# A linear attention's output products in halves of the depth, in pairs on the two halves of the array's rows, with a PSUM bank for each half

## The chip, the cores and the metric

The kernel runs on one core of a Trainium2 chip, written in Bass and Tile. The metric is the device time of one execution in microseconds, median of the runs shown. Its result must agree with the reference in fp32.

## What is computed

One layer of a decoder: 1024 tokens of width 1024, a wide input projection, then two branches side by side, softmax attention with latent queries and keys (8 heads) and a gated linear attention (4 heads), a gated merge, an output product and gated embeddings. The part that matters here is the linear attention:

```python
def step(state, inp):                      # per head, chunk by chunk
    qi, ki, vi, bi = inp                   # bi: running sum of the log decay
    o_inter = einsum('bhcd,bhde->bhce', qi * exp(bi), state)
    ...
    attn = einsum('bhid,bhjd,bhijd->bhij', qi, ki, decay)
    o = o_inter + einsum('bhij,bhje->bhie', attn, vi)
    ...
```

The kernel takes chunks of 128 tokens. For each head and chunk the output is a sum of two products: the chunk's decayed scores times its values (depth 128, the chunk's tokens), and the decayed queries times the state that the earlier chunks left (depth 64, the head's width). The first chunk has no state.

## The kernel before

The dense products (`bank`, line 149) are made of three products each (`mm3`, lines 144 to 147: high by high, high by low, low by high part of the operands), 128 rows deep and 512 columns wide; a bank is 24 of them, or 8 steps of depth. They run as a stream of tiles (`stream`, line 158), the next tile's weights loaded one tile ahead (`load_w`: a DMA, a copy of the high part on ScalarE, line 127, and the low part on VectorE, line 128). The input projection's last 25 tiles fill the time of the linear attention, from 116 to 440 us: `steps` (line 733) runs `gla(t, h)` for the four pairs of a half `h` of the tokens and a pair `t` of heads, and after each `yield` in it one dense bank is issued (lines 740 and 741). The framework then puts the instructions of each engine in an order by a model of the time, so a bank may be moved a little; on each engine the order is fixed when the kernel runs.

A call of `gla` handles two heads and four chunks in ten steps. It makes the states (`pu`, line 586); the scores in six parts, merged into the tile `at` by VectorE (lines 637 and 641), each part by products on 64 rows, one head in rows 0 to 63 and the other in rows 64 to 127 (`cross`, line 555, alternates the heads, each head with a PSUM bank of its own); then, in one step, the outputs: for each head a PSUM bank `po`, and per chunk a product of `at` with the values (line 684, 128 rows) and one of `qe` with the state (line 700, 64 rows). ScalarE copies the bank out (line 702) and squares it with sums by token (line 706). The next step turns the sums into the norm's factor (`newton`, VectorE), the one after scales on GpSimd (line 717) and transposes back on TensorE (line 720).

PSUM has eight banks of 512 fp32 columns. In this stage (line 454) two are for dense products (`d`), four for two score tiles of two banks each (`L`), one for an output (`o`) and one for the rest (`u`: transposes, states). `o` is used once more, for the sums of a latent's norm (line 788).

Of the kernel before, what the change touches and what calls it, by code (L numbers as in the profile page):

```python
# [11 lines left out]
AF = mybir.ActivationFunctionType  # L12
# [4 lines left out]
P = 128  # L17
# [11 lines left out]
# columns of the packed gain vectors  # L29
V_IN, V_Q, V_KV, V_BGK, V_GLA, V_PLE, V_PG, V_FIN = 0, 8, 11, 13, 15, 16, 24, 32  # L30
NVEC = 40
# columns of the float constants
# [7 lines left out]
def _pieces(v):  # L40
    """v as a sum of two numbers of 12 bits and a float."""
    a = np.float64(v)
    out = []
    for _ in range(2):
        m, e = math.frexp(a)
        p = math.ldexp(round(math.ldexp(m, 12)), e - 12)
        out.append(p)
        a = a - p
    out.append(float(np.float32(a)))
    return out  # L50


def hybrid_kernel(tc, a, out):
# [3 lines left out]
    with ExitStack() as ctx:  # L57
# [72 lines left out]
        def split_gain(dst_hi, dst_lo, src, g):  # L130
            """the two parts of src * g, g per partition"""
            nc.scalar.activation(dst_hi, src, AF.Copy, scale=g)  # L132
            nc.vector.scalar_tensor_tensor(dst_lo, src, g, f(dst_hi), op0=ALU.mult, op1=ALU.subtract)  # L133
# [15 lines left out]
        def bank(get, hi, lo, w, c0, kts, xh, xl, h, evict, tag="d"):  # L149
            """out[w features, half h of the tokens] with the weights' k-tiles at c0 + kt * w."""  # L150
            ps = get(tag, "d")
            n = len(kts)
            for i, kt in enumerate(kts):
                c = slice(c0 + kt * w, c0 + kt * w + w)
                mm3(ps[:w], hi[:, c], lo[:, c], xh[kt][:, hs(h)], xl[kt][:, hs(h)], i == 0, i == n - 1)
            evict(h, ps)

        def stream(get, jobs, xh, xl, primed=None, ahead=1, order=None):
            """Dense tiles, the next one's weights always on their way; yields after the first
            load and after each bank.  # L160
            A job: (source, columns of a k-tile, k-tiles, evict)."""
# [25 lines left out]
        def newton(dst, ss, n, w):  # L187
            """dst = rsqrt(ss / n + EPS), [128, w]"""
# [14 lines left out]
        def newton1(dst, s1, s2, n):  # L203
            """dst = rsqrt((s1 + s2) / n), [128, 1]; v is half the argument, the iterates change sign"""
# [13 lines left out]
        def rstd_rows(get, tag, acc, n, r):  # L218
            """From acc[128, tokens] (sums of squares by partition) the rstd of token block tb in r[128, 8]."""
            pr = get(tag, "ss")  # L220
            for tb in range(8):
                nc.tensor.matmul(pr[:, tb : tb + 1], acc[:, tb * P : (tb + 1) * P], ones[:, 0:1], start=True, stop=True)
            newton(r, pr[:, :8], n, 8)

        def rstd_parts(r):
            """both parts of r [128, 8]"""
            rh, rl = small("rh", 8, F32R, bufs=2), small("rl", 8, bufs=2)
            nc.scalar.activation(rh, r, AF.Copy)
            nc.vector.tensor_tensor(rl, r, f(rh), op=ALU.subtract)
            return f(rh), rl  # L230

        def rstd_bcast(get, tag, parts, h):
            """[128, 512] in PSUM: rstd of each token of half h along the free axis, on every partition."""
# [20 lines left out]
        # =====================================================================  # L254
        # The input projection. Its operand is x * g; the token's rstd comes in
        # where a product leaves PSUM.
        # =====================================================================
# [14 lines left out]
        with tc.tile_pool(name="ps0", bufs=1, space=PSUM) as ps0:  # L272
# [20 lines left out]
            # the array reaches its full clock only under load: it gets some while the first loads are on their way  # L293
# [4 lines left out]
            # x * g in two parts, and the sums of squares  # L298
# [53 lines left out]
            # constants of the linear attention  # L352
# [4 lines left out]
            # the gate's second product in one pass: rows 64.. hold the operands' parts  # L357
            # (hi, hi, lo, lo) and (hi, lo, hi, lo)
# [10 lines left out]
            # gate chain: the running sums of log sigmoid within a chunk  # L369
# [22 lines left out]
            # rope tables: cos, and sin with its sign. A tile of rope's rows holds four heads'  # L392
            # first halves, then their second halves.
            cs = [alloc(F32, "cs") for _ in range(2)]

            def rope_tables():
# [23 lines left out]
                # the key's: parts in rows 0.. and 32.., halves of them in rows 64.. and 96..  # L420
# [12 lines left out]
            # values of the linear attention, by token  # L433
# [14 lines left out]
        # =====================================================================  # L448
        # Linear attention, between the tiles of the rest of the projection
        # =====================================================================  # L450
        with tc.tile_pool(name="psG", bufs=1, space=PSUM) as psG:
            gctx = ExitStack()
            gp = gctx.enter_context(tc.tile_pool(name="gtmp", bufs=NG))
            get = psum_pool({"d": (HALF, 2), "L": (S, 2), "o": (HALF, 1), "u": (HALF, 1)}, psG)
# [44 lines left out]
            # latents: raw, and their sums of squares  # L499
# [31 lines left out]
            def gla(t, h):  # L531
                """Pair of heads t, half h: four chunks of 128 tokens."""
# [34 lines left out]
                # decayed keys, by token, and the chunks' states  # L567
# [41 lines left out]
                # the chunks' own scores, transposed, level by level  # L609
# [43 lines left out]
                # neighbours and the diagonal  # L653
# [19 lines left out]
                # outputs by token, their norm, and back  # L673
                ss = small("gss", 8)
                oss = []
                prev = None
                for hd in range(2):
                    po = get("o", "o")
                    e0 = (2 * t + hd) * P
                    for c in range(4):  # L680
                        tb = 4 * h + c
                        cs = slice(c * P, (c + 1) * P)
                        st = states[c]
                        i1 = nc.tensor.matmul(
                            po[:, cs],
                            at[:, hd * HALF + c * P : hd * HALF + (c + 1) * P],
                            vtok(tb)[:, e0 : e0 + P],
                            start=True,
                            stop=st is None,
                        )  # L690
                        if c:
                            tc.add_manual_dep(
                                i1.ins,
                                prev.ins.name,
                                mybir.DependencyInfo(mybir.DependencyClass.NoSync, mybir.DependencyReason.DATA),
                                reason="one group at a time in a bank",
                            )
                        prev = i1
                        if st is not None:
                            prev = nc.tensor.matmul(po[:, cs], qe[rows(hd), cs], st[rows(hd), :], start=False, stop=True)  # L700
                    os_ = g2("os")
                    nc.scalar.activation(os_, po, AF.Copy)
# [45 lines left out]
            # the gated outputs in two parts  # L748
# [39 lines left out]
            kvh, kvl = finish_latent(get, "o", "L", "ckv", 256, V_KV)  # L788
# [8 lines left out]
        # =====================================================================  # L797
        # Softmax attention
        # =====================================================================
        with tc.tile_pool(name="psB", bufs=1, space=PSUM) as psB:  # L800
# [15 lines left out]
            def rope_queries(g):  # L816
                """Rope's rows of four heads' queries, in two parts to DRAM."""
# [18 lines left out]
            def make_pair(pr):  # L836
                """Queries and keys of two heads, without rope in rows 0.. of the first's and rows
                64.. of the second's; rope's rows 64..95, and 0..63 twice (the keys' halved)."""
# [35 lines left out]
            # values, by token, packed [hi | lo] per head  # L874
# [58 lines left out]
            def weighted(hn, hf, pq, sl, rc4):  # L933
# [3 lines left out]
                # the gate over the softmax's sums, these as rows by way of DRAM  # L937
# [65 lines left out]
            def parts(pr, h):  # L1003
                """both parts of heads' pair pr, half h"""
# [7 lines left out]
            # per-layer embeddings, by token, times their gain; half the norm's factor in re  # L1012
# [91 lines left out]
        # =====================================================================  # L1104
        # Merge, output product, gated embeddings, final norm
        # =====================================================================
        with tc.tile_pool(name="psC", bufs=1, space=PSUM) as psC:
# [7 lines left out]
            # x2 = x + merged @ w_out: its parts times the gain by feature, itself by token  # L1115
# [56 lines left out]
            def block(tb, b, c0, w, et):  # L1172
                """Columns c0 .. c0 + w of block b's; they start at column o of the row."""
# [28 lines left out]
            for tb in range(8):  # L1202
                # all but the row's last piece, and their sum with the guard's share
# [21 lines left out]
def _tiles(w, cols, width=P):  # L1225
    """[K, M] -> rows of m-tiles, each [128, K / 128 * width]: partition = k within its tile."""
# [30 lines left out]
def _layout(inputs):  # L1257
# [21 lines left out]
    # rope's columns, by four heads: the first halves, then the second halves  # L1279
# [35 lines left out]
```

## Time and profile before

| | us |
|---|---|
| three runs: median | 996.18 |
| lowest, highest | 995.36, 997.62 |
| span of the profiled execution | 995.6 |
| TensorE busy (matmuls) | 968.8 (97%) |
| VectorE busy | 585.0 (59%) |
| ScalarE busy | 413.4 (42%) |
| GpSimd busy | 127.8 (13%) |
| linear attention's stretch | 116 to 440 |

The time of a run is that of the whole execution; the span is from the first to the last instruction in the one execution that was profiled. A product in fp32 shows as two records of a matmul and two of a weight load. A matmul's record is longer than the distance to the next one, since they are pipelined: read distances from start to start.

### The profile page before, as it was taken

How to read it: one execution, taken by the hardware profiler on the slowest of the kernel's cores; microseconds unless marked ns; L12 is line 12 of the kernel's file. 1: busy time of each engine (PE TensorE's matmuls, PEld its weight loads, DVE VectorE, ACT ScalarE, POOL GpSimd, SP SyncE). 2: the span in 40 equal slices, each digit the busy share in tenths (PEclk: the TensorE clock that was granted, in tenths of full speed). 3: DMA queues.
4: the chain of work that ended last, by engine and by line, in shares of the span. 5: the costliest groups of instructions: out<-in, count | busy, mean ns of one | idle time of the engine just before them, and what ended most of it. 6: DMA issues, size and time to landing. Idle time of an engine off the chain costs nothing. (4 is left out here: it accounts for less than half of the span.)

```text
span 995.6 us, 13955 instructions
## 1 busy us (share of the span) xinstructions
PE 968.8 (97%) x5152; PEld 801.1 (80%) x5152; DVE 585.0 (59%) x1219; ACT 413.4 (42%) x800; POOL 127.8 (13%) x103
## 2 busy tenths in 40 slices
PE   7999999999999999999999999997999999999996
PEld 5787778887887788788888788886888778889985
DVE  6727764375364355342567568885756862238766
ACT  7316721332331332221233246785886432237333
POOL 2100000000000000001111022234454000000322
PEclk9999999999999999999999999998999999999999
DMA  7300111122232122130162844537146762135212
GB/s 277 93 22 22 64 43 43 58 80 86 75 106 79 60 85 75 54 114 24 54 204 89 230 131 121 150 94 180 59 149 212 245 221 74 43 106 181 74 64 106
DMA packets 47827, 105.68 MB, mean 106 GB/s; under 512 B 6736, under 2 KB 9616, under 8 KB 47760
## 3 DMA queue, kind: packets, MB, share of 16 engines
q1 hardware_dynamic: 47760, 104.81, 32.9%
q8 instruction: 40, 0.66, 0.3%
q14 instruction: 27, 0.22, 0.1%
HBM read 72.18 MB, written 25.20 MB: 98 GB/s over the span
## 5 line engine op out<-in xcount | busy, mean ns | idle before, releaser
L145 PE MATMUL d<-xh,wh 128*128 128x512 f32 x544 | 215.4, 399 | 3.1 <-ACT xh L132 3.0
L146 PE MATMUL d<-xl,wh 128*128 128x512 f32 x544 | 214.1, 394 | 0.1
L147 PE MATMUL d<-xh,wl 128*128 128x512 f32 x544 | 213.8, 394 | 0.1
L145 PEld LDWEIGHTS d<-xh,wh 128*128 128x128 f32 x544 | 102.7, 189 | 28.2 <-ACT xh L132 4.9
L128 DVE TENSOR_TENSOR wl<-wr,wh 128x1024 fp32r<-128x1024 f32 (+2 forms) x59 | 73.6, 1249 | 86.9 <-ACT wh L127 66.7
L146 PEld LDWEIGHTS d<-xl,wh 128*128 128x128 f32 x544 | 102.9, 189 | 22.0 <-DVE xl L133 0.8
L147 PEld LDWEIGHTS d<-xh,wl 128*128 128x128 f32 x544 | 102.7, 189 | 22.2 <-DVE wl L128 0.5
L127 ACT ACTIVATE wh<-wr 128x1024 fp32r<-128x1024 f32 (+4 forms) x81 | 76.3, 943 | 105.5 <-DMA wr<-in_w_in 35.8
L145 PE MATMUL pg<-wh,gh 128*128 128x256 f32 (+1 forms) x200 | 62.7, 314 | 0.0
L146 PE MATMUL pg<-wl,gh 128*128 128x256 f32 (+1 forms) x200 | 62.5, 313 | 0.0
L147 PE MATMUL pg<-wh,gl 128*128 128x256 f32 (+1 forms) x200 | 62.5, 313 | 0.0
L128 DVE TENSOR_TENSOR pt<-pt,pt 128x512 fp32r<-128x512 f32 (+1 forms) x96 | 51.5, 551 | 16.1 <-ACT pt L127 15.7
L924 ACT ACTIVATE p<-p,nm 128x128 f32<-128x128 f32 (+3 forms) x64 | 49.3, 772 | 21.8 <-DVE nm L914 21.7
L494 ACT ACTIVATE z<-z 128x512 f32<-128x512 f32 x32 | 20.1, 629 | 91.1 <-DVE z L466 85.3
L466 DVE TENSOR_TENSOR z<-d,rb 128x512 f32<-128x512 f32 x32 | 22.0, 688 | 50.9 <-PE d L147 50.9
L145 PE MATMUL d<-mh,wh 128*128 128x512 f32 x128 | 50.9, 400 | 0.6 <-ACT mh L127 0.6
L127 ACT ACTIVATE pt<-pt 128x512 fp32r<-128x512 f32 (+1 forms) x96 | 44.6, 485 | 15.5 <-PE pt L963 14.0
L146 PE MATMUL d<-ol,wh 128*128 128x512 f32 x128 | 50.1, 393 | 0.4 <-DVE ol L128 0.4
L147 PE MATMUL d<-mh,wl 128*128 128x512 f32 x128 | 50.2, 392 | 0.0
L147 PE MATMUL d<-oh,wh 128*128 128x512 f32 x128 | 50.0, 392 | 0.0
L146 PE MATMUL d<-ml,wh 128*128 128x512 f32 x128 | 49.9, 390 | 0.0
L145 PE MATMUL d<-oh,wh 128*128 128x512 f32 x128 | 49.9, 395 | 0.0
(262 smaller groups left out, 1938.5 us busy)
## 6 DMA issues: line engine op xcount, KB each, us to landing
wr<-in_w_in SPq DMA_DIRECT2D x33, 512.0 KB
d_ta<-z SPq DMA_DIRECT2D x16, 256.0 KB
d_tb<-z SPq DMA_DIRECT2D x16, 256.0 KB
tb<-d_tb SPq DMA_DIRECT2D x16, 256.0 KB
d_zb<-tb SPq DMA_DIRECT2D x16, 256.0 KB
d_e<-er SPq DMA_DIRECT2D x16, 256.0 KB
ta<-d_ta SPq DMA_DIRECT2D x16, 256.0 KB
zb<-d_zb SPq DMA_DIRECT2D x16, 256.0 KB
```

Source lines behind the costliest of these rows:

```text
L127: nc.scalar.activation(dst_hi, src, AF.Copy)
L128: (eng or nc.vector).tensor_tensor(dst_lo, src, f(dst_hi), op=ALU.subtract)
L145: nc.tensor.matmul(ps, lh, rh, start=first, stop=False)
L146: nc.tensor.matmul(ps, lh, rl, start=False, stop=False)
L147: nc.tensor.matmul(ps, ll, rh, start=False, stop=last)
L466: nc.vector.tensor_tensor(z, ps, rb[:, hs(h)], op=ALU.mult)
L494: nc.scalar.activation(z, z, AF.Tanh, scale=0.5)
L924: nc.scalar.activation(pt[:, :w], pt[:, :w], AF.Exp, bias=nm, scale=-1.0, accum_out=den)
```

## The change

The output step's PSUM bank per head becomes a tile of two banks for each half of the depth, `po[0]` and `po[1]`, taken from the `L` buffers: `po[k]` holds what rows `64k` to `64k + 63` contribute, one head in its first bank and the other in its second. The score product of depth 128 is divided in two of depth 64. Per chunk the order is head 0 on rows 0 to 63 and head 1 on rows 64 to 127; head 0 on rows 64 to 127 and head 1 on rows 0 to 63; then, where there is a state, each head's state product on its own rows. VectorE adds the two halves after ScalarE's copy of the first. The bank `o` goes to the dense products, which have three, and the latent's sums use `u`. In all other places the diff only takes out comments and docstrings.

```diff
-            get = psum_pool({"d": (HALF, 2), "L": (S, 2), "o": (HALF, 1), "u": (HALF, 1)}, psG)
+            get = psum_pool({"d": (HALF, 3), "L": (S, 2), "u": (HALF, 1)}, psG)
...
-                prev = None
+                po = [get("L", "o") for _ in range(2)]
+                prev = {}
+                for c in range(4):
+                    tb = 4 * h + c
+                    cs = slice(c * P, (c + 1) * P)
+                    st = states[c]
+                    for part in range(2 if st is None else 3):
+                        for hd in range(2):
+                            k2 = hd ^ (part == 1)
+                            r, hc = rows(k2), slice(hd * HALF + c * P, hd * HALF + (c + 1) * P)
+                            e0 = (2 * t + hd) * P
+                            lt, rt = (at[r, hc], vtok(tb)[r, e0 : e0 + P]) if part < 2 else (qe[r, cs], st[r, :])
+                            i1 = nc.tensor.matmul(po[k2][:, hc], lt, rt, start=part < 2, stop=part == 2 or st is None or k2 != hd)
+                            if (k2, hd) in prev:
+                                tc.add_manual_dep(
...
+                            prev[k2, hd] = i1
                 for hd in range(2):
-                    po = get("o", "o")
-                    e0 = (2 * t + hd) * P
-                    for c in range(4):
...
-                        i1 = nc.tensor.matmul(
-                            po[:, cs],
-                            at[:, hd * HALF + c * P : hd * HALF + (c + 1) * P],
-                            vtok(tb)[:, e0 : e0 + P],
-                            start=True,
-                            stop=st is None,
-                        )
...
-                        if st is not None:
-                            prev = nc.tensor.matmul(po[:, cs], qe[rows(hd), cs], st[rows(hd), :], start=False, stop=True)
                     os_ = g2("os")
-                    nc.scalar.activation(os_, po, AF.Copy)
+                    nc.scalar.activation(os_, po[0][:, hs(hd)], AF.Copy)
+                    nc.vector.tensor_tensor(os_, po[1][:, hs(hd)], os_, op=ALU.add)
...
-            kvh, kvl = finish_latent(get, "o", "L", "ckv", 256, V_KV)
+            kvh, kvl = finish_latent(get, "u", "L", "ckv", 256, V_KV)
```

## Rows read from the trace of the kernel before

**Rows 1.** The page: busy time by engine, and TensorE's busy tenths in 40 slices.
```profile
PE 968.8 (97%) x5152; PEld 801.1 (80%) x5152; DVE 585.0 (59%) x1219; ACT 413.4 (42%) x800; POOL 127.8 (13%) x103
...
PE   7999999999999999999999999997999999999996
```

**Rows 2.** Stretch, length; busy PE, PEld, DVE, ACT, POOL; granted clock; DMA share, GB/s.
```profile
116.00:440.00 324.00, 323.78 (x1877) 259.44 (x1876) 167.02 (x308) 99.12 (x194) 12.17 (x16) 1.00 0.21 72
```

**Rows 3.** Timeline of TensorE, outputs of half 0: start, length, instruction, merged count.
```profile
176.07 0.39 PE L147 MATMUL d<-xh,wl 128*128 128x512 f32 x1
...
177.25 0.49 PE L684 MATMUL o<-gqkv,at 128*128 128x128 f32 x2
...
178.08 0.49 PE L684 MATMUL o<-gqkv,at 128*128 128x128 f32 x2
...
178.92 0.50 PE L145 MATMUL d<-xh,wh 128*128 128x512 f32 x1
179.25 0.40 PE L146 MATMUL d<-xl,wh 128*128 128x512 f32 x1
```

**Rows 4.** The same timeline around a group of outputs of half 1.
```profile
327.31 0.39 PE L145 MATMUL d<-xh,wh 128*128 128x512 f32 x1
...
330.76 0.50 PE L146 MATMUL d<-xl,wh 128*128 128x512 f32 x1
331.10 0.40 PE L147 MATMUL d<-xh,wl 128*128 128x512 f32 x1
```

**Rows 5.** The same timeline around eight products of scores (16 records).
```profile
168.18 0.39 PE L145 MATMUL d<-xh,wh 128*128 128x512 f32 x1
...
168.63 0.39 PE L147 MATMUL d<-xh,wl 128*128 128x512 f32 x1
...
170.04 0.50 PE L145 MATMUL d<-xh,wh 128*128 128x512 f32 x1
170.38 0.39 PE L146 MATMUL d<-xl,wh 128*128 128x512 f32 x1
```

**Rows 6.** The timeline with windows that end early: the first records of two groups.
```profile
176.30 0.49 PE L684 MATMUL o<-gqkv,at 128*128 128x128 f32 x3
176.30 0.60 PE L684 MATMUL o<-gqkv,at 128*128 128x128 f32 x4
168.95 0.49 PE L559 MATMUL L<-rq,rk 64*128 64x128 f32 x4
168.95 1.05 PE L559 MATMUL L<-rq,rk 64*128 64x128 f32 x14
```

**Rows 7.** Groups by line, count, busy us, mean ns, idle time before and its releaser.
```profile
L702 ACT ACTIVATE os<-o 128x512 f32<-128x512 f32 x8 | 4.8, 599 | 30.1 <-PE o L700 30.1
L706 ACT ACTIVATE junk<-os 128x128 f32<-128x128 f32 x32 | 9.5, 299 | 0.2
L466 DVE TENSOR_TENSOR z<-d,rb 128x512 f32<-128x512 f32 x32 | 22.0, 688 | 50.9 <-PE d L147 50.9
```

**Rows 8.** Timelines of TensorE and GpSimd behind two groups of outputs.
```profile
186.68 0.50 PE L146 MATMUL d<-xl,wh 128*128 128x512 f32 x1
194.84 2.04 POOL L717 TENSOR_TENSOR os<-os,grs 128x512 f32<-128x512 f32 x2 [44.46 <-DVE grs L200]
...
416.11 0.50 PE L147 MATMUL d<-xh,wl 128*128 128x512 f32 x1
420.73 2.04 POOL L717 TENSOR_TENSOR os<-os,grs 128x512 f32<-128x512 f32 x2 [41.55 <-DVE grs L200]
426.68 0.60 PE L720 MATMUL oT<-ident,os 128*128 128x128 f32 x4
```

**Rows 9.** Waits by total: who waited for whom, us, times, longest.
```profile
DVE wl L128 <- PE o L684: 20.1, 2, 10.7
```

**Rows 10.** TensorE's longest wait in the softmax attention, and the stretch behind (as in 2).
```profile
690.33 0.42 PE L145 MATMUL s<-kh,qh 96*128 96x128 f32 x1 [5.17 <-DMA kl<-kl]
690.40:700.50 10.10, 9.48 (x37) 8.71 (x37) 5.75 (x21) 6.95 (x16) 6.67 (x4) 0.50 0.56 171
```

More of the change, by code (lines that the diff above doesn't have):

```diff
@@ L675, in gla @@
                 oss = []
-                prev = None
-                for hd in range(2):
-                    po = get("o", "o")
-                    e0 = (2 * t + hd) * P
-                    for c in range(4):
-                        tb = 4 * h + c
-                        cs = slice(c * P, (c + 1) * P)
-                        st = states[c]
-                        i1 = nc.tensor.matmul(
-                            po[:, cs],
-                            at[:, hd * HALF + c * P : hd * HALF + (c + 1) * P],
-                            vtok(tb)[:, e0 : e0 + P],
-                            start=True,
-                            stop=st is None,
-                        )
[L691 to L698, printed above, removed]
-                        if st is not None:
-                            prev = nc.tensor.matmul(po[:, cs], qe[rows(hd), cs], st[rows(hd), :], start=False, stop=True)
@@ new lines, in gla @@
+                po = [get("L", "o") for _ in range(2)]
[13 more added lines that the diff above has]
+                                tc.add_manual_dep(
+                                    i1.ins,
+                                    prev[k2, hd].ins.name,
+                                    mybir.DependencyInfo(mybir.DependencyClass.NoSync, mybir.DependencyReason.DATA),
+                                    reason="one group at a time in a bank",
+                                )
+                            prev[k2, hd] = i1
```

## The prediction

> **What bounds the kernel now.** I read the page first: TensorE's matmuls are busy for 97% of the span and of the forty slices only the first, the last and one at 685 to 710 us fall under 9 tenths, while VectorE is at 59% and ScalarE at 42% [rows 1]. Matmuls overlap in their pipeline, so "busy" alone doesn't prove a bound. The table by stages does better: in the linear attention's stretch, 116 to 440 us, TensorE is busy for 323.78 of 324.00 us at full granted clock, VectorE for 167 us and ScalarE for 99 us [rows 2]. In that stretch TensorE never waits for anything that counts; what stands in its queue sets the time. So a microsecond taken out of TensorE's queue there is a microsecond off the end, provided that nobody else then comes late, and that the later stages, where TensorE is as busy in nearly every slice [rows 1], are simply pushed forward.
>
> Next I read the output products one by one, in order of time. What counts is the distance from start to start, not the duration of a record. Each fp32 product shows as two records. Dense products follow each other by 0.225 us (168.18 to 168.63, with one more start between, is 0.45 us) [rows 5]. A group of output products (one head, four chunks) is bounded by the last dense start ahead of it and the second dense start behind it; two normal distances (0.45 us) are taken off.
>
> - Half 0 of the tokens, where the first chunk has no state and so no second product: 176.07 to 179.25 is 3.18 us, less 0.45 is 2.73 us [rows 3]. There are four such groups.
> - Half 1, with all eight products: 327.31 to 331.10 is 3.79 us, less 0.45 is 3.34 us [rows 4]. Four of these too.
>
> The sum is 4 x 2.73 + 4 x 3.34 = 24.3 us of the span's 995.6.
>
> Where do they go? Records of 128 rows that follow each other start every 0.11 us: the first three end 0.49 us after the group's start and the first four 0.60 us [rows 6]. A chunk with both products has four records and would take 0.44 us at that rate, but 177.25 to 178.08 is 0.83 us [rows 3]. The missing 0.39 us goes at the two places where the queue changes between a product on 128 rows (line 684) and one on 64 rows (line 700): about 0.2 us for each change of form, and there are 6 in a group of half 0 and 8 in one of half 1, counting the return to the dense products.
>
> **What the change takes and adds on TensorE.** The new group holds both heads. It has only products on 64 rows, those on rows 0 to 63 alternating in pairs with those on rows 64 to 127: per chunk 4 halves of the score product and 2 state products. That makes 22 products in half 0 and 24 in half 1, four groups in all. Every second neighbour is of the same half (the order is 0 1, 1 0, 0 1), but taken two by two each pair lies on different halves and in different PSUM banks.
>
> The trace has this form already: `cross` issues 8 products on 64 rows, heads alternating. From the last dense start (168.63) to the second one behind (170.38) is 1.75 us, less 0.45 is 1.30 us for the eight, both changes of form included [rows 5]. Within it, ten more records take 1.05 - 0.49 = 0.56 us [rows 6], so 0.056 us a record and 0.112 us a product, which is half of a 128-row product's. So a new group costs 1.30 + (22 - 8) x 0.112 = 2.87 us in half 0 and 1.30 + (24 - 8) x 0.112 = 3.09 us in half 1. Two of each: 11.9 us.
>
> TensorE gives back 24.3 - 11.9 = **12.4 us**. Cutting the score product in two halves earns nothing by itself: two halves at 0.112 cost what one whole product at two records of 0.11 costs. Of the 12.4 us about 3 are the 28 state products, which now run in pairs (28 x 0.11), and the rest is changes of form: 4 x 6 + 4 x 8 = 56 before, two for each new group, 8, after.
>
> Bounds: if nothing overlapped within a new group, a record would cost 0.11 us, and 44 or 48 records plus the 0.40 us of entry and exit (1.30 - 16 x 0.056) would be 5.24 and 5.68 us; together 21.8 us, a gain of 2.4 us. Above, nothing in the rows is faster than `cross`. I take `cross`, since the form (64x128), the alternation and the two banks are the same.
>
> **What it adds elsewhere.** ScalarE's eight copies of 0.60 us stay. VectorE gets eight additions of a 128x512 PSUM tile and an SBUF tile; the nearest row, the dense evictions of that shape, is 0.69 us [rows 7], so 5.5 us in a stretch where VectorE is free for 157 us. They cost nothing as long as two things hold. First, the squares (line 706) now wait for the addition and the ScalarE queue behind them waits too: what is queued there are the ScalarE half of weight splits and the tanh of dense evictions. The work that hides such delays is the dense products themselves. How much they hide a wait shows: VectorE stood 20.1 us in two pieces, 10.7 us the longer, in front of a weight split, for line 684's last reading of the score tile [rows 9], and TensorE still lost only 0.22 us in the whole stretch. So a delay of 0.7 us is covered; if that cover were gone, eight of them would cost 5.5 us, and I count 0. (The 20.1 us shrink too, since both heads now finish together.) Second, the transposes of line 720 must still find their operand ready; that is the rival below.
>
> PSUM: both `L` buffers are taken by the new output tile. They were last read by the fourth and fifth merges of scores, and the output products need the fifth merge anyway, so no new wait on entry. The next user of `L` is the next pair's first scores, four steps (four banks of dense work) later. The third `d` bank has no wait to remove, since TensorE waits for none [rows 2]; I count it at nothing. So is the move of the latent's sums to the bank `u`, long after its last user.
>
> **The rivals.**
>
> *The halves don't overlap in this order.* Twice per chunk two neighbours use the same rows. The trace's only example alternates strictly. The Trainium skill (TensorE: Matmul & The Clock Gate, What overlaps and what doesn't) says that weight loads overlap matmuls in flight only where the rows differ and that matmuls keep strict order; taken strictly, that speaks for this rival, and no row here shows the order 0 1 1 0. Time: 996.2 - 2.4 = 993.8 us. Against it: pairs counted from the chunk's start never share rows. 7 in 100.
>
> *The eviction becomes the bound.* The Trainium skill (TensorEngine Tiling, PSUM Bottleneck) warns that tiling speeds up TensorE and not the emptying of PSUM. In rows: the scaling on GpSimd began 194.84 - 186.68 = 8.2 us after the last output product in the slowest group and 420.73 - 416.11 = 4.6 us in the quickest [rows 8]. To that come the first head's copy and squares, which ran beside dense work between the two heads before (0.60 + 4 x 0.30 = 1.8 us by [rows 7]), two additions (1.4 us) and the first scaling itself (1.0 us): the first transpose can go 8.8 to 12.4 us after the products. Its cover was 426.68 - 416.11 = 10.6 us at least [rows 8] and is by the order of the steps two banks, 2 x 24 x 0.225 = 10.8 us, to which the 5 us of dense work that stood between the two heads may come. So at worst 1.5 to 2 us in some of four groups, a time of 984 to 990 us: 9 in 100.
>
> *Slower than before* by the same place: if the transposes were queued behind one bank only (5.4 us), TensorE would stand 3.4 to 7.0 us in each of four groups, 14 to 28 us, and the time would be 998 to 1012 us. It decides from 3.1 us of wait per group (12.4 / 4). Against it: the steps put two banks in between, and the shortest distance in the trace is 10.6 us. 3 in 100.
>
> *A later wait shifts.* In the softmax attention TensorE once stands 5.17 us for a copied key tile, and the granted clock is 0.50, the 1.2 GHz level, for 10 us from there [rows 10]. All of it moves forward with the rest, but the order there may come out a little different: without it up to 5 us of wait and the 5 us that half the clock costs less (974), with a second one 10 us more (994). 4 in 100 each way.
>
> **How the numbers follow.** Likeliest, 73 in 100: 12.4 us off. The profiled span is 995.6 us and the median of three runs 996.18, so 0.6 us lies around it; 996.2 - 12.4 = 983.8 us, its own range 981 to 987. The range of 8 in 10 reaches down to 979 (half of the later wait gone) and up to 992 (eviction waits, part of the overlap missing). A change within 0.2% (2 us), about what a measurement of this kernel can tell from none, needs the first rival at its worst or waits that eat the gain: 3 in 100. Slower: 3 in 100. Faster: 94 in 100.
>
> **What would show it.** The steps are right if the groups of output products come as four runs of 44 or 48 records on 64 rows that take 2.7 to 2.9 us from the first to the next dense start, with TensorE's work up to the end of the last group shorter by some 12 us and no wait ahead of line 720's transposes. Records 0.11 us apart would mean the first rival; gaps on TensorE ahead of the transposes the second. An equal or longer span with short groups would make the whole argument wrong: TensorE's queue would not have been the bound.

## The result and the profile after

The changed kernel takes 984.96 us (median of 4 runs, 983.49 to 988.31), the kernel before 995.77 us beside it. The ratio is 0.9893, 95% interval 0.9869 to 0.9916: about 1.1% faster. Forecast were 983.8 us and a range of 979 to 992. Two later repetitions of the changed kernel gave 987.9 and 984.84 us, ratios 0.991 and 0.9877.

The page of the changed kernel: busy time by engine, and TensorE's busy tenths in 40 slices.

```profile
PE 955.8 (97%) x5216; PEld 794.3 (81%) x5216; DVE 590.2 (60%) x1227; ACT 413.1 (42%) x800; POOL 128.1 (13%) x103
...
PE   7999999999999999999999999997999999999995
```

TensorE has 64 records more and 13 us less of busy time than in [rows 1]; its picture by slices is the same but for the last digit. That it still bounds the linear attention's stretch is read from its idle time there, below. VectorE has 5 us more, the eight additions.

The timeline of TensorE in the changed kernel (start, length, instruction, merged count; in brackets the wait before and what ended it): the last record of the stage before the linear attention, a group of outputs of each half, the first transposes behind one, the first record of the stage after, the product behind the long wait in the softmax attention, and a product at which the clock is back.

```profile
115.36 0.39 PE L147 MATMUL gv<-wh,xl 128*128 128x512 f32 x1
...
175.70 0.39 PE L147 MATMUL d<-xh,wl 128*128 128x512 f32 x1
176.01 1.16 PE L690 MATMUL o<-gqkv,at 64*128 64x128 f32 x16
177.01 0.39 PE L690 MATMUL o<-st,qe 64*128 64x128 f32 x4
...
178.67 0.50 PE L145 MATMUL d<-xh,wh 128*128 128x512 f32 x1
179.00 0.39 PE L146 MATMUL d<-xl,wh 128*128 128x512 f32 x1
...
193.32 0.60 PE L720 MATMUL oT<-ident,os 128*128 128x128 f32 x4
...
321.82 0.39 PE L145 MATMUL d<-xh,wh 128*128 128x512 f32 x1
325.02 0.50 PE L146 MATMUL d<-xl,wh 128*128 128x512 f32 x1
325.36 0.39 PE L147 MATMUL d<-xh,wl 128*128 128x512 f32 x1
...
508.57 0.39 PE L145 MATMUL v<-wh,ch 128*128 128x512 f32 x1
...
678.01 0.44 PE L145 MATMUL s<-kh,qh 96*128 96x128 f32 x1 [5.53 <-DVE pt L128]
...
688.14 0.48 PE L145 MATMUL s<-kh,qh 96*128 96x512 f32 x1
```

Read as [rows 3] and [rows 4] were, from the last dense start to the second dense start behind, less 0.45: 179.00 - 175.70 - 0.45 = 2.85 us in half 0, 325.36 - 321.82 - 0.45 = 3.09 us in half 1. All four groups together are 11.88 us, where the eight of before were 24.28. The same two outer records in the kernel before, and the last product:

```profile
115.70 0.39 PE L147 MATMUL gv<-wh,xl 128*128 128x512 f32 x1
...
521.05 0.40 PE L145 MATMUL v<-wh,ch 128*128 128x512 f32 x1
...
700.46 0.55 PE L145 MATMUL s<-kh,qh 96*128 96x512 f32 x1
```

Between the first two lies the whole linear attention with its dense work: 521.05 - 115.70 = 405.35 us before, 508.57 - 115.36 = 393.21 us after. The gain is there, 12.14 us. Below this distance is called the GLA stretch.

Two stretches of the changed kernel (length; busy PE, PEld, DVE, ACT, POOL; granted clock; DMA share, GB/s):

```profile
116.00:440.00 324.00, 323.77 (x1993) 262.13 (x1992) 174.62 (x319) 101.12 (x198) 12.13 (x16) 1.00 0.21 76
...
674.43:688.09 13.66, 9.42 (x35) 8.68 (x36) 6.03 (x21) 8.54 (x19) 7.28 (x4) 0.50 0.70 176
```

The first answers to [rows 2]: no wait has come in, at 0.23 us of idle time against 0.22. The second answers to [rows 10]: at the long wait the granted clock is at the 1.2 GHz level for 13.66 us here, for 10.2 us in the profile of before. The longer stretch holds no more work: 3.58 us of it (674.43 to 678.01) lie inside the wait, where TensorE stands, and from the product behind the wait to the product at which the clock is back both kernels take 10.13 us (688.14 - 678.01 and 700.46 - 690.33).

### The profile page after: what moved, and what is told of

It reads as the page before. It is cut to its first block, busy times and chain, and to the rows that moved or that the text cites. A ratio compares the mean times of both kernels' runs of the same rounds, so it can differ in the third digit from the quotient of the medians.

```text
span 981.7 us, 14101 instructions
## 1 busy us (share of the span) xinstructions
PE 955.8 (97%) x5216; PEld 794.3 (81%) x5216; DVE 590.2 (60%) x1227; ACT 413.1 (42%) x800; POOL 128.1 (13%) x103
## 4 chain that ended last, share of the span: by engine, by line
PE 86%; DVE 6%; ACT 3%; DMA 3%; issue 2%; SPq 0%; DVEq 0%; ACTq 0%
PE d L145 19%; PE d L147 18%; PE d L146 18%; PE pt L963 3%; PE pg L147 3%; PE pg L146 3%; PE pg L145 3%; PE L L559 2%; PE o L955 2%; PE s L146 2%; PE o L954 2%; PE s L147 2%; PE s L145 2%; PE o L690 1%; DMA kl<-kl 1%
## 5 line engine op out<-in xcount | busy, mean ns | idle before, releaser
L127 ACT ACTIVATE pt<-pt 128x512 fp32r<-128x512 f32 (+1 forms) x96 | 44.6, 485 | 15.5 <-PE pt L963 13.6
```

The lines of the kernel that those rows point to most:

```text
L127: nc.scalar.activation(dst_hi, src, AF.Copy)
```

## The experiments

Each kernel was run beside the kernel before (four chips, 68 runs of it, medians 996.56 to 997.61 us). Group sums and GLA stretches are read as above.

| kernel | median, us | ratio, 95% interval | output groups, us | GLA stretch, us |
|---|---|---|---|---|
| before | 996.6 to 997.6 | 1 | 24.28 | 405.35 |
| the change, again | 987.90 | 0.9886 to 0.9934 | 11.88 | 393.24 |
| the change, a third time | 984.84 | 0.9849 to 0.9904 | 11.88 | 393.23 |
| e1, no pairs | 997.95 | 0.9985 to 1.0025 | 20.78 | 402.28 |
| e2, sorted by form | 988.57 | 0.9879 to 0.9945 | 13.62 | 395.17 |
| e3, sorted, state products in pairs | 985.31 | 0.9866 to 0.9908 | 11.88 | 393.57 |
| e4, longer eviction | 984.88 | 0.9846 to 0.9897 | 11.88 | 392.87 |
| e5, PSUM layout alone | 998.37 | 0.9996 to 1.0032 | 24.28 | 405.39 |
| e6, e7, keys first by order of the text | 987.75, 998.49 | 0.9883 to 0.9932, 0.9996 to 1.0028 | 11.88, 24.28 | 393.23, 405.31 |
| e8, e9, keys first by edges | 982.61, 1000.21 | 0.9833 to 0.9884, 0.9997 to 1.0046 | 11.88, 24.28 | 393.38, 407.78 |
| e10, e3 with e8's order | 987.13 | 0.9879 to 0.9932 | 11.88 | 393.56 |

The theory: three prices make up the groups, 0.112 us for a record (two make a product), half of that where neighbours lie on different rows, 0.2 us for a change of form, between products on 128 and on 64 rows. Rivals: the pairs bring nothing and the forms all of it, or the reverse; the PSUM layout brings a part; the eviction costs a part.

**The change again.**

> The changed kernel once more, beside the three below. Theory (TensorE's queue is the bound, the output groups shrink from 24.3 to 11.9 us and nothing else comes late): output groups 2.85 and 3.09 us each, time 12.4 us under the kernel before. If the stretch at half clock in the softmax attention is what differs between executions, the difference can read between 8 and 15 us, with the spans following the length of that stretch and not the output groups.

> The changed kernel itself, beside e10 on one chip: 985 to 988 us, output groups 11.9 us in sum.

The groups and the stretch repeat to 0.05 us. The time as a whole doesn't: 984.96, 987.90, 984.84. What moves is behind the stretch: from its end to the end of the span it is 473.2, 477.2 and 477.3 us in the three profiles of the change, 474.6 us in that of before. e6 to e10 are on that. The spans don't follow the stretch at half clock (the 1.2 GHz level), as the first expectation held possible: of the three profiles the shortest span has the longest one.

**e1: the same 64-row products, first all on rows 0 to 63, then all on rows 64 to 127.**

```diff
-                for c in range(4):
...
-                        for hd in range(2):
-                            k2 = hd ^ (part == 1)
+                for k2 in range(2):
+                    for c in range(4):
...
+                            hd = k2 ^ (part == 1)
```

> The changed kernel's products in another order: all on rows 0 to 63 first, then all on rows 64 to 127; same number, same banks, same additions, same two changes of form per group. Theory that pairs on the two row halves run at once: a record every 0.11 us and not every 0.056, groups of 5.2 and 5.7 us, 9.9 us more in sum than the changed kernel, so only 2.4 us under the kernel before. Rival that the fewer changes of form are the whole gain and pairs don't matter: groups of 2.9 and 3.1 us, time of the changed kernel.

Nearly the whole gain is gone: 20.78 us for the groups, a time that can't be told from before. So pairing is what makes the halved products pay, 20.78 - 11.88 = 8.9 us. The expectation was 1 us too high, and the timeline of e1 (first group) shows why:

```profile
175.02 0.39 PE L147 MATMUL d<-xh,wl 128*128 128x512 f32 x1
...
177.23 0.71 PE L690 MATMUL o<-gqkv,at 64*128 64x128 f32 x6
177.68 0.27 PE L690 MATMUL o<-st,qe 64*128 64x128 f32 x1
177.78 0.27 PE L690 MATMUL o<-gqkv,at 64*128 64x128 f32 x1
177.79 0.27 PE L690 MATMUL o<-st,qe 64*128 64x128 f32 x1
...
180.44 0.39 PE L146 MATMUL d<-xl,wh 128*128 128x512 f32 x1
```

TensorE's queue holds all 22 records on rows 0 to 63 ahead of the 22 on rows 64 to 127. The last two of the first rows are the state product's at 177.68 and 177.79. A score record of the other rows (177.78) stands between them, and the six at 177.23 are two more than the last chunk's four. So the records run over the seam between the two: the second rows' first records start beside the last three of the first rows. That saves 3 x 0.112 = 0.34 us a group, and 44 x 0.112 + 0.40 - 0.34 = 4.99 us, against the 4.97 that the group takes (180.44 - 175.02 - 0.45).

**e2 and e3: whole score products on 128 rows first, then the state products;** in e2 head 0's and then head 1's, in e3 alternating. The state products have a PSUM tile of their own, and VectorE's addition leaves out the first chunk of half 0, which has only its score products. The second and third added lines are e2's and e3's form of one line.

```diff
+                for part in range(2):
+                    for c, hd in [(c, hd) for hd in range(2) for c in range(4)]:
+                    for c, hd in [(c, hd) for c in range(4) for hd in range(2)]:
...
+                        lt, rt = (at[:, hc], vtok(tb)[:, e0 : e0 + P]) if part == 0 else (qe[rows(hd), cs], st[rows(hd), :])
+                        i1 = nc.tensor.matmul(po[part][:, hc], lt, rt, start=True, stop=True)
```

> Score products left whole (128 rows), both heads' eight first, then the state products, head 0's and then head 1's, so not in pairs; scores and state products in PSUM tiles of their own, added by VectorE as in the change. Three changes of form a group instead of twelve to sixteen, nothing halved, nothing paired. Theory (a change of form costs 0.2 us): groups of 28 x 0.11 + 0.6 = 3.7 and 32 x 0.11 + 0.6 = 4.1 us, 15.6 us in sum, 8.7 us under the kernel before. Rival that halving and pairing is where the gain comes from: groups near 2 x 2.7 and 2 x 3.3 us, time of the kernel before.

> As the one before, but the state products alternate between the heads and so between the row halves: the whole score products, with only the state products in pairs. Theory (halving a 128-row product earns nothing, pairing two 64-row products saves 0.11 us each): groups of 16 x 0.11 + 12 x 0.056 + 0.6 = 3.0 and 16 x 0.11 + 16 x 0.056 + 0.6 = 3.3 us, 12.6 us in sum, within 1 us of the changed kernel and 3 us under the run before this one. Rival that two halves in pairs are quicker than one whole product: 3 to 7 us more than the changed kernel.

The first group on TensorE's timeline, of e2:

```profile
176.06 0.39 PE L147 MATMUL d<-xh,wl 128*128 128x512 f32 x1
176.29 1.95 PE L690 MATMUL o<-gqkv,at 128*128 128x128 f32 x16
178.17 1.26 PE L690 MATMUL o<-st,qe 64*128 64x128 f32 x12
179.36 0.50 PE L145 MATMUL d<-xh,wh 128*128 128x512 f32 x1
179.70 0.40 PE L146 MATMUL d<-xl,wh 128*128 128x512 f32 x1
```

and of e3:

```profile
176.21 0.39 PE L147 MATMUL d<-xh,wl 128*128 128x512 f32 x1
176.44 1.95 PE L690 MATMUL o<-gqkv,at 128*128 128x128 f32 x16
178.31 0.94 PE L690 MATMUL o<-st,qe 64*128 64x128 f32 x12
179.18 0.50 PE L145 MATMUL d<-xh,wh 128*128 128x512 f32 x1
179.52 0.40 PE L146 MATMUL d<-xl,wh 128*128 128x512 f32 x1
```

e3 takes what the change takes, 11.88 us: eight whole score products cost what sixteen paired halves cost, and cutting them in two earns nothing. Its rows also give the price of a change of form. The score products start 176.44 - 176.21 = 0.23 us after the dense one, the normal distance, so dense to whole score is no change; there are two, in and out of the 64-row form. 2.86 = 16 x 0.112 + 12 x 0.056 + 2 x 0.20. The price is not one of adding up in PSUM. In the kernel before each state product adds to the score product just ahead of it; in e3 nothing is added in PSUM across a change of form, and it costs the same. In e2 the same twelve records without pairs would cost 0.67 us more; they cost 0.32 more (3.18), again less by three records that overlap at the seam between the heads. Its expectation was high by this and by one change of form too many. The difference between e2 and before, 24.28 - 13.62 = 10.7 us, is then 48 changes of form fewer (9.3 us, at the 0.194 us that 56 of them cost before: (24.28 - 120 x 0.112) / 56) and the overlap at four seams (4 x 0.34 = 1.4 us): sorting by form alone, with no pair by intent, brings most of what the change brings.

**e4: two more copies on ScalarE and two on VectorE for each head, between the addition and the squares.**

```diff
                     nc.vector.tensor_tensor(os_, po[1][:, hs(hd)], os_, op=ALU.add)
+                    for _ in range(2):
+                        nc.scalar.activation(os_, os_, AF.Copy)
+                        nc.vector.tensor_copy(os_, os_)
```

> The changed kernel with a longer eviction: after VectorE's addition the output tile is copied onto itself twice by ScalarE and twice by VectorE, for each head, some 4 to 5 us more on the way from the output products to the transposes of line 720. In the changed kernel GpSimd's scaling begins 8.8 to 9.6 us after the last product, and the first transpose stands 13.3 to 14.7 us after it. Theory (the addition is hidden with 3 to 5 us to spare): no wait of TensorE ahead of line 720, or under 1 us in a group, time of the changed kernel within 2 us. Rival (the eviction is at its bound): 4 to 5 us more in each of four groups, 16 to 20 us, slower than the kernel before.

TensorE's waits of e4 in 116 to 440 us (us in total, times, longest) are one:

```profile
PE d L145 <- ACT wh L127: 0.2, 1, 0.2
```

The first scaling on GpSimd, in the changed kernel and in e4:

```profile
187.57 2.04 POOL L717 TENSOR_TENSOR os<-os,grs 128x512 f32<-128x512 f32 x2 [37.58 <-DVE grs L200]
```

```profile
190.86 2.49 POOL L720 TENSOR_TENSOR os<-os,grs 128x512 f32<-128x512 f32 x2 [40.52 <-DVE grs L200]
...
196.38 0.60 PE L723 MATMUL oT<-ident,os 128*128 128x128 f32 x4
```

The groups of outputs end at 178.67 and 179.02, so the scaling begins 8.9 us behind the products in the changed kernel and 11.8 us in e4. That is 2.9 us more, and 1.7 to 2.2 us in the other three groups, where 4 to 5 were expected. The transposes came 14.7 us behind in the one and 17.4 us in the other: the framework, which knows of the added copies, queued them later, and dense work fills the place (76 records of it ahead of the first transpose where there were 64). The eviction is no bound, and 1.7 to 2.9 us more of it cost nothing. This doesn't show what happens if the chain is longer than the framework believes.

**e5: the PSUM layout of the change, with the products of before.**

```diff
-            get = psum_pool({"d": (HALF, 2), "L": (S, 2), "o": (HALF, 1), "u": (HALF, 1)}, psG)
+            get = psum_pool({"d": (HALF, 3), "L": (S, 2), "u": (HALF, 1)}, psG)
...
+                po2 = get("L", "o")
...
-                    po = get("o", "o")
+                    po = po2[:, hs(hd)]
```

> The kernel before with the change's PSUM layout alone: three banks for dense products, the outputs of both heads in one L tile, the latent's sums in u; the products as before, score and state in turn. Theory (TensorE waited for no bank): groups of the two heads together 5.4 and 6.7 us as before, time of the kernel before within 2 us. Rival (the third dense bank is part of the gain): 3 us or more under it.

Groups and stretch are those of before; the third dense bank and the moved sums are worth nothing.

**e6 to e10: where the rest of the time comes from.** In the softmax attention the copies of a pair's key tiles stand on SP's queue behind rope rows of the queries, which wait for a copy of the queries to land (in the changed kernel the copy is issued at 661.8 us and the first rope row at 668.4). The theory was that this makes the wait of 5.2 to 5.5 us and the stretch at half clock. e6 (on the changed kernel) and e7 (on the kernel before) issue the key copies earlier in the text:

```diff
+                for x in "qk":
+                    for y in range(2):
+                        t1 = f(qk[x + "hl"[y], 2 * pr + 1])
...
```

> The changed kernel with one edit in the softmax attention: for a pair of heads the copies of the keys are issued ahead of the rope rows of the second head's queries, which made the copy queue stand 6 us for an earlier copy. Theory (what lies between the 12.4 us of the linear attention and the 9 to 11 us of the medians is the wait for the third pair's keys and the half clock behind it, whose length differs between executions): that wait falls from 5 us to under 1.5, the half-clock stretch behind it goes, 5 to 10 us under the changed kernel. Rival (the wait is set by the keys' products, not by the queue): no difference.

> The kernel before with that same edit. Theory: 5 to 10 us under the kernel before, and 12.4 us (11 to 14) over the run before this one, since the change's gain no longer passes through a wait that varies. Rival (the medians' 9 to 11 us are the true gain, the rest being lost in the later stages whatever they wait for): 9 to 11 us over it.

They tell nothing on the theory: the framework put the copies where they had been (in e6 at 673.16 and 674.25 us, behind the rope rows at 669.48), and the wait stayed. e8 (on the changed kernel) and e9 (on the one before) hold the rope rows back with ordering edges:

```diff
+                    late.append((t1[r + 16 * s_ : r + 16 * s_ + 16], d_[s_]))
+                for o_, i_ in late:
+                    w = nc.sync.dma_start(o_, i_)
+                    tc.add_manual_dep(w.ins, copy.ins.name, ..., reason="key copies first")
```

> The changed kernel with one thing more: in make_pair the rope rows of the odd head's queries are written after both key copies of the pair, and an ordering edge holds them there, so that on SP's queue the key copies no longer stand behind writes that wait about 7 us for a query copy to land (in the changed kernel's profile the last pair: query copies issued at 661.1 and 661.8, rope rows at 668.4 to 671.5, key copies at 672.1 and 673.2). Theory (the wait of 5.5 us at the last pair's scores and the half-clock stretch of 13.7 us behind it come from the late key copies): key copies issued at 668 to 670, the wait 0.5 to 2.5 us, the half-clock stretch gone, the span from the first score product to the last 155 to 160 us where it was 164.2, the time 976 to 981 us where the changed kernel has 985 to 988. Rival (the keys are held by the eviction of their own bank, the order on the queue is nothing): key copies after 671.5, the wait 4 us or more, 984 to 988 us. Output groups of linear attention unchanged, 11.9 us.

> The kernel before with the same order held by edges. Theory: its wait of 5.17 us and its 10.2 us at half clock go as well, 5 to 9 us off, 988 to 992 us; the difference to the changed kernel with this order is then that of the linear-attention stretch alone, 12.1 us, with less spread than between the kernels without it. Rival: 995 to 999 us.

SP's queue in the changed kernel, and ScalarE:

```profile
668.38 1.72 SPq L871 DMA_DIRECT2D qh<-d_rq  x4
...
671.07 0.42 SPq L137 DMA_DIRECT2D wr<-in_pT  x1
...
672.06 0.47 SPq L864 DMA_DIRECT2D kh<-kh  x1
673.15 0.47 SPq L864 DMA_DIRECT2D kl<-kl  x1
...
676.00 1.06 ACT L127 ACTIVATE wh<-wr 128x1024 fp32r<-128x1024 f32 x1 [3.63 <-DMA wr<-in_pT]
```

and SP and TensorE in e8:

```profile
666.84 0.33 SPq L137 DMA_DIRECT2D wr<-in_pT  x1
...
668.87 0.46 SPq L865 DMA_DIRECT2D kh<-kh  x1
669.95 0.71 SPq L865 DMA_DIRECT2D kl<-kl  x1
...
672.86 0.30 PE L145 MATMUL s<-kh,qh 96*128 96x128 f32 x1 [0.54 <-DVE pt L128]
...
741.34 0.49 PE L963 MATMUL o<-pt,vp 128*128 128x512 f32 x1 [1.34 <-ACT pt L127]
742.98 0.50 PE L964 MATMUL o<-pt,vp 128*128 128x512 f32 x1 [1.14 <-DVE pt L128]
...
744.61 0.63 PE L145 MATMUL d<-oh,wh 128*128 128x512 f32 x1
745.04 0.63 PE L146 MATMUL d<-ol,wh 128*128 128x512 f32 x1
```

That the rope rows ahead on the queue make the wait is shown: with them held back the copies are 3.2 us earlier, the wait is 0.54 us instead of 5.53, there is no half clock behind it, and the span from the first score product to the last 153.98 us instead of 164.17. Which of the transfers behind the rope rows ends the wait isn't shown. e8 also moved another load of this queue forward, that of `in_pT` for the embeddings, from 671.07 to 666.84 us. In the changed kernel's profile ScalarE stood 3.63 us for it, ahead of its part in splitting the transposed attention weights (`pt`), and the profile puts the end of TensorE's wait down to `pt` and not to the keys. In the kernel before and in the two repetitions of the change the same wait is put down to a key copy.

But the gain isn't kept: from the last score product to the first of the embeddings' gate (`pg`), 175.4 us instead of 167.9. New waits stand there, for the split of `pt`, and a stretch at half clock (744.0 to 747.4 us) in which dense products follow each other every 0.43 us instead of 0.225. On the kernel before, the same order ended at 1000.21 us: its long wait went too, and instead of one stretch at half clock of 10.2 us there are four of 3.4 us, three of them in other places. The first lies in the GLA stretch, which is 2.4 us longer. That expectation was wrong.

> The order of the copy queue from e8 (rope rows of the odd head's queries behind both key copies) with the products of e3 (whole score products, state products in pairs). The GLA stretch as in e3, 393.6 us, and the wait for the last pair's keys at 1 us or less as in e8. Theory (form of the score products is nothing, the order takes 3 to 5 us off): 980 to 985 us, 3 to 5 us below the changed kernel in the same call. Rival (the difference of e8 to the changed kernel was between chips only): 985 to 988 us, level with the changed kernel here.

e10 ran on the same chip as the changed kernel: 987.13 beside 984.84 us. e3's products, which e10 has, were level with the change's, so the order brings nothing there. Its two longest waits in 650 to 760 us:

```profile
PE rcT L949 <- DVE rc L937: 3.1, 1, 3.1
PE o L964 <- ACT pt L127: 3.0, 2, 2.8
```

They have taken the place of the wait for the keys. e8's 982.61 us is the lowest median here, but with e10 beside it I don't count it as a version that beats the change.

Each run has its span and its mean granted clock. Their product counts time at half clock as half, whether TensorE works in it or stands; the rest of the span is the most that the lower clock can have cost. Means over all runs, with two standard errors:

| | runs | span x clock, us | the rest, us |
|---|---|---|---|
| before | 68 | 985.9 ± 0.4 | 9.6 ± 0.5 |
| the change (three times) | 15 | 973.9 ± 1.0 | 10.6 ± 0.8 |
| e1 | 12 | 984.3 ± 0.8 | 12.3 ± 1.1 |
| e3 | 6 | 973.9 ± 0.8 | 9.7 ± 1.2 |
| e8 | 5 | 976.0 ± 0.8 | 4.9 ± 1.1 |
| e9 | 12 | 990.2 ± 0.7 | 8.2 ± 1.4 |
| e10 | 6 | 978.7 ± 1.1 | 6.9 ± 2.1 |

The change takes 12.0 ± 1.1 us off the first column, which is the GLA stretch, and 1.0 ± 0.9 us comes on in the second. That is not shown to be a cost of the lower clock: a good part of the second column is time in which TensorE stands. In the profile of before TensorE works in 9.6 of 15.1 us at half clock, in the three of the change in 9.4 of 20.6, 9.8 of 20.8 and 8.0 of 17.3 us. Besides the waits, the last 4.9 us of the span before and the last 6.9 to 7.1 us after have the lower clock and no work for TensorE. The order of e8 to e10 takes 1 to 6 us off the second and puts 2 to 5 us on the first. The mean time of the change is 11.0 ± 1.3 us under that of before. What stays open is why the place and number of the half-clock stretches differ from run to run of one kernel.

## Why the prediction was right

- *TensorE's queue is the bound in the stretch.* Right: 12.40 us less in the groups, 12.14 us less in the stretch; in e1, e2 and e3 the stretch is shorter than before by 3.07, 10.18 and 11.78 us where the groups are shorter by 3.50, 10.66 and 12.40. 0.3 to 0.6 us of each gain is lost between the groups, about what the score products take more: dense work parts them into 24 pieces in the change and e1 and into 25 in e2 and e3, where before there are 22, and read as the output groups are they take 31.4 and 31.6 us where they took 31.0.
- *The price of a pair, from `cross` [rows 5, 6].* Right: 2.87 and 3.09 us forecast, 2.85 and 3.09 measured. The order 0 1, 1 0, 0 1 overlaps as the strict alternation does; the rival that it doesn't is out.
- *0.2 us for a change of form.* Right, and e3's rows show it without the pairs. The Trainium skill (TensorEngine Tiling, Key Properties) says that changing the tiling mode drains TensorE; the trace agrees so far as each change costs time, 0.20 us here.
- *Halving the score products earns nothing by itself.* Right: e3. The split of the 12.4 us, 9.3 for the changes of form and 3.1 for the state products' pairs, was right as a sum of prices. As a statement of what happens without pairs it was short: e2 loses 1.74 us, not 3.1, since the seam overlaps by itself.
- *The additions cost nothing.* Right: they take 0.68 us each (0.69 forecast), and the wait of [rows 9] is gone.
- *The eviction rival.* Right in its working: the first scaling begins 8.5 to 9.6 us behind the products and takes 1.0, so the first transpose could go at 9.5 to 10.7, within the 8.8 to 12.4 worked out; the transposes come 13.3 to 14.7 us behind, more than the 10.8 of the two banks. e4 puts it out.
- *The PSUM layout costs and brings nothing.* Right: e5.
- *All later work moves forward unchanged.* Right to about 1 us, which the runs hardly tell from none: 11.0 ± 1.3 us in the mean for the 12.4 forecast, of which 0.3 are missing in the stretch. Behind it the profiles differ in waits rather than in the clock. TensorE's waits there are 10.9 us before and 10.4, 13.6 and 14.8 us in the three of the change, and the time goes with them (474.6; 473.2, 477.2 and 477.3 us). At half clock TensorE works about as long as before (9.6; 9.4, 9.8 and 8.0 us). Why the waits differ from run to run stays open. The prediction had the long wait as a rival with 5 to 10 us either way; it shifts a little in nearly every run instead. That 984.96 us lies within 1.2 us of 983.8 is in part luck: one kernel's medians lie 3 us apart.
- *A slip in reading.* The one slice of [rows 1] under 9 tenths in the middle is the 28th, at 672 to 697 us and not at 685 to 710. The long wait of [rows 10], from 685.2 to 690.3 us, lies in either, and nothing else hangs on it.

## What to carry to other kernels

Where TensorE is the bound, count its changes between products on 128 and on 64 rows before anything else: sorting products by form gave 10.7 of the 12.4 us here (e2, with 1.4 of them from the overlap at the seams), and needs no cut product. Products on 64 rows cost half only in neighbours on different rows; cut in two and issued without pairs, they gave back nearly all (e1). Before a wait on a copy queue is moved, look at which work stands right behind it: e8 took 10.2 us out of the score products' span and lost 7.5 of them again behind it, at the next operand.

## What the runs showed of the hardware

Queued records on other rows start before the last three on the first rows have started: 0.34 us saved at each seam, in e1 and e2, in both halves of the tokens. The Trainium skill (TensorE: Matmul & The Clock Gate, What overlaps and what doesn't) says that matmuls keep their order at start and end; for the start the trace of e1 disagrees, by the score record at 177.78 us ahead of the state record at 177.79, and by the two score records too many that started before 177.68.

In e8 the granted clock falls to the 1.2 GHz level at 744.0 us, 1.0 us after the second of two waits (1.34 and 1.14 us, 0.5 us of work between them). It falls at other places in other executions of one kernel: at 674.43 us in one profile of the change, at 552.19 and 678.48 us in another. A change that only moves waits moves the time at half clock too, by 1 to 6 us in the second column here, which is as much as the intervals of these comparisons are wide. Only the part in which TensorE works can cost anything: of the 13.66 us at the long wait that is 9.42 us.
